# Pooling sums of all four groups on VectorE, issued one by one, and the decay and beta projection in two passes over 32 stationary columns

## The chip, the cores and the metric

The kernel runs on one NeuronCore of a Trainium2 chip. The metric is the device time of one execution in microseconds (us), lower is better. Five engines work in parallel, each through its own instructions in order: PE (TensorE, matrix products), DVE (VectorE), ACT (ScalarE), POOL (GpSimd) and SP (SyncE, which here only issues transfers). An instruction waits where another engine or a transfer has not yet delivered.

## The reference

One transformer-like layer is applied to 128 context tokens and to 1024 latent tokens (a grid of 16 rows by 64 columns). What matters here are two branches of its mixing part, both fed from one normalised and modulated input `h`:

```python
qkv, z, a, b, u, gate_a, gate_b = _split_cols(h @ w_in)
...
g = -jnp.exp(a_log) * jax.nn.softplus(a4 + dt_bias)   # log-decay, 8 columns of the projection
beta = jax.nn.sigmoid(b4)                             # 8 more columns
...
for gi, w in enumerate(POOL_WINDOWS):                 # windows 2, 4, 8, 16
    ug = uf[:, :, gi]                                 # 128 channels each
    if grid_w is None:
        m = _window_mean(ug, w, 1)
    else:
        m = _window_mean(_window_mean(grid, w, 2), w, 1)
    outs.append(m - ug)
y = jnp.einsum('btgc,gcd->btgd', d, w_pool)
```

The pooling branch takes, for each of four groups of 128 channels, the mean over a centred window (along the context sequence, and along both axes of the latent grid), subtracts the value itself, and multiplies by a 128 by 128 matrix per group. The decays and the betas are 16 columns of the same input projection. All tensors are 32-bit floats.

## The kernel before, in words

All 1152 tokens lie along the free axis of tiles of 128 channels, in three chunks of 384 tokens. A product of 32-bit precision is made from three matmuls in a faster format: each operand is split into a rounded part and a rest (`hi`, `lo`), and hi times hi, hi times lo and lo times hi are added in PSUM (`gemm`, lines 499 to 501). A split is an ACT copy (`whi`, L157) and a subtraction on DVE (`wlo`, L158). Three PSUM banks (`psg`, tag "g") take the chunks in turn; a chunk's matmuls wait until the evacuation of the chunk three before it is done.

The order on every engine is the order in which the Python code issues instructions. `gemm_stream` gives the order of the products that the prediction speaks of: the pooling inputs `u` of groups 3, 2, 1, 0 (`u_task`), the decay and beta projection (`ab_task`), q, k and v of head 0 (`conv_task`, each 24 steps of three matmuls, with a five-tap convolution on DVE behind it), the pooling projection (`pool_proj`), and then the product of its result with `w_b_proj` (`yb_task`). After the products for groups 1 and 0, for ab, q, k and v stands a modulation step (`with_mod`: `mod_step`, 16 matmuls of a vector with a part of `w_mod`, L386; DVE copies its result to `part`, L388). Then SP loads the next part of `w_mod` (four transfers of 512 KB, tile `wm`, L264) into the same four tiles. Behind the projection of ab two small matmuls (`modr`, L409) make a row that DVE finishes in four operations (`gra`, L411 and L412) and SP stores (`grow_d`, L413); the next four `wm` loads stand behind that store in SP's queue.

VectorE work that has no fixed place waits in a queue `bg`: every second step of a `gemm` takes one entry from its front and issues it. The pooling sums of groups 2, 1 and 0 (windows 8, 4, 2) are such entries, the convolution taps are appended behind them (L541). A group's sums are doublings: two zeroed pads and a copy, then log2(window) additions, for the context, for two halves of the grid along the columns, and for two halves along the rows; then a product with the reciprocal counts (`rc`, loaded by SP, L602; L630) and the subtraction of the input. Group 3 (window 16) instead is issued at once, all 35 instructions, on GpSimd (`pool_group(g, u, POOL, now)`). `pool_split` makes `dh` and `dl` of a group's result; `pool_proj` drains the queue until three groups are split, splits group 3, and multiplies the groups in the order 2, 1, 0, 3: 12 chunks of three matmuls, evacuated by `scaled` in turn by ACT (L193) and by DVE (L198, tile `sp`).

Of the kernel before, what the change touches and what calls it, by code (L numbers as in the profile page):

```python
# [79 lines left out]
def hybrid_layer(ctx: ExitStack, tc: tile.TileContext, ins, outs, dbg=None):  # L80
# [66 lines left out]
    def w_split():  # L147
        i = wstate["split"]
        if i >= len(wq):
            return  # L150
        while wstate["raw"] <= i:
            w_load()
        wstate["split"] += 1
        t, n = wraw.pop(i)
        hi = wts.tile([P, 1024], F32R, tag="hi", bufs=2, name=f"whi{i}")
        lo = wts.tile([P, 1024], F32R, tag="lo", bufs=2, name=f"wlo{i}")
        ACT.activation(out=hi[:, 0:n], in_=t[:, 0:n], func=AF.Copy)  # L157
        lo_eng[0].tensor_tensor(out=lo[:, 0:n], in0=t[:, 0:n], in1=hi[:, 0:n].bitcast(F32), op=ALU.subtract)  # L158
        wsplit[i] = (hi, lo)
# [79 lines left out]
    with tc.manual_schedule():  # L239
# [276 lines left out]
        def conv_task(dst, m):  # L516

            pb = pad[pad_i[0] % 2]
            pad_i[0] += 1
            taps[m] = 4  # L520

            def evac(c, o):
                if c == 0:
                    while old and taps[old]:
                        bg.popleft()()
                    ACT.copy(out=pb[:, 2:130], in_=o[:, 0:128])
                    ACT.copy(out=pb[:, 132:388], in_=o[:, 128:384])
# [42 lines left out]
        d_act = {}  # L570
        d_raw = {}

        def window_sum(q, x, y, n, w, pos, out):

            p = w // 2
            a, b = x, y
            v = 2
            while v <= w:
                r = w // 2 - v // 2
                s, e = p - r, p + n + r  # L580
                d = v // 4
                lo, hi = (s - 1, s) if v == 2 else (s - d, s + d)
                o = out if v == w else pos(b, s, e)
                q("tensor_tensor", out=o, in0=pos(a, lo, lo + e - s), in1=pos(a, hi, hi + e - s), op=ALU.add)
                a, b = b, a
                v *= 2

        def pool_group(g, u, eng, queue):
            w = WINDOWS[g]
            p = w // 2  # L590

            def q(f, **kw):
                queue.append(lambda: getattr(eng, f)(**kw))

            rcb = []
            s = slot(name="plS")
            t0 = slot(name="plA")
            t1 = slot(name="plB")

            def rc_load():  # L600
                rcb.append(slot(name="rc"))
                SP.dma_start(out=rcb[0][:, 0:T], in_=I["rc"][g:g + 1].to_broadcast([P, T]))  # L602

            def pads(lo, hi, **kw):
                def f():
                    eng.memset(lo, 0.0)
                    eng.memset(hi, 0.0)
                    eng.tensor_copy(**kw)
                queue.append(f)

            pads(t0[:, 0:p], t0[:, p + T_CTX:p + T_CTX + p], out=t0[:, p:p + T_CTX], in_=u[:, 0:T_CTX])
            window_sum(q, t0, t1, T_CTX, w, lambda t, a, b: t[:, a:b], s[:, 0:T_CTX])
            LW = GRID_W + w
            for half in range(2):
                nr = GRID_H // 2
                a0 = T_CTX + half * nr * GRID_W
                va, vb = v3(t0, nr, LW), v3(t1, nr, LW)
                pads(va[:, :, 0:p], va[:, :, p + GRID_W:LW], out=va[:, :, p:p + GRID_W], in_=v3(u, nr, GRID_W, a0))
                window_sum(q, va, vb, GRID_W, w, lambda t, a, b: t[:, :, a:b], v3(s, nr, GRID_W, a0))
            LH = GRID_H + w  # L620
            grid = v3(s, GRID_H, GRID_W, T_CTX)
            for half in range(2):
                ncol = GRID_W // 2
                va, vb = v3(t0, LH, ncol), v3(t1, LH, ncol)
                cs = slice(half * ncol, (half + 1) * ncol)
                if half == 1:
                    queue.append(rc_load)
                pads(va[:, 0:p], va[:, p + GRID_H:LH], out=va[:, p:p + GRID_H, :], in_=grid[:, :, cs])
                window_sum(q, va, vb, GRID_H, w, lambda t, a, b: t[:, a:b, :], grid[:, :, cs])
            queue.append(lambda: eng.tensor_tensor(out=s[:, 0:T], in0=s[:, 0:T], in1=rcb[0][:, 0:T], op=ALU.mult))  # L630
            q("tensor_tensor", out=s[:, 0:T], in0=s[:, 0:T], in1=u[:, 0:T], op=ALU.subtract)
            d_raw[g] = s
            if eng is DVE:

                queue.append(lambda: queue.insert(min(12, len(queue)), lambda: pool_split(g)))

        def pool_split(g):
            s = d_raw.pop(g)
# [4 lines left out]
        def u_task(g, early=None):  # L643
            u = slot(name="u")

            def evac(c, o):
                ACT.copy(out=u[:, c * CH:(c + 1) * CH], in_=o)

            if early is None:
                yield from gemm(8, h_at, evac)  # L650
            else:
                w, acc = early
                for c, o in enumerate(acc):
                    evac(c, o)
# [12 lines left out]

        abt = []

        def ab_task():  # L670
            abt.append(slot(name="ab"))
            abs_ = abt[0][0:16]

            def evac(c, o):
                ACT.copy(out=abs_[:, c * CH:(c + 1) * CH], in_=o)

            yield from gemm(8, h_at, evac, m=16)

        gcol = {}
        gc_d = dram.tile([72, P], F32, name="gc_d")  # L680

        def gate_prep(fill):
            pt = psd("abT")
            abs_ = abt.pop()[0:16]
            for c in range(NT):
                PE.transpose(pt[:, c * 16:(c + 1) * 16], abs_[:, c * P:(c + 1) * P], ident[0:16, 0:16])
# [4 lines left out]
            ab = pt[:, 0:144].rearrange("p (c j) -> p j c", j=16)  # L691

            def col(name):
                t = const.tile([P, 72], F32, name=name)
# [7 lines left out]
            xa, ax, e, s2, q, t1 = (gp[:, 72 * i:72 * i + 72] for i in range(6))  # L702
            sums, gr = gp[:, 432:432 + 3 * P], gp[0:72, 816:816 + P]
            SP.dma_start(out=sums, in_=I["sums"])
            beta = col("beta")
            fill(2500)
            DVE.tensor_tensor(out=w3(xa), in0=ab[:, 0:8, :], in1=bc_last(dtb, NT), op=ALU.add)
# [1587 lines left out]
```

## Time and profile before

| | |
|---|---|
| median of 3 runs | 1802.12 us (1800.2 to 1806.25) |
| profiled execution, its own time | 1805.9 us |
| span of that execution in the trace | 1804.1 us |
| PE busy, share of the span | 93% |
| DVE, ACT, POOL busy | 64%, 40%, 42% |
| mean granted clock of PE | 0.972 of full speed |

All positions in time below are microseconds from the start of the span. The profiled execution took 1.8 us more than its span, and 3.8 us more than the median of the runs. A busy PE means that matmuls overlap without a gap in the trace; whether it advances at full speed is seen from the distance between the starts of two matmuls.

### The profile page before, as it was taken

How to read it: one execution, taken by the hardware profiler on the slowest of the kernel's cores; microseconds unless marked ns; L12 is line 12 of the kernel's file. 1: busy time of each engine (PE TensorE's matmuls, PEld its weight loads, DVE VectorE, ACT ScalarE, POOL GpSimd, SP SyncE). 2: the span in 40 equal slices, each digit the busy share in tenths (PEclk: the TensorE clock that was granted, in tenths of full speed). 3: DMA queues.
4: the chain of work that ended last, by engine and by line, in shares of the span. 5: the costliest groups of instructions: out<-in, count | busy, mean ns of one | idle time of the engine just before them, and what ended most of it. 6: DMA issues, size and time to landing. Idle time of an engine off the chain costs nothing.

```text
span 1804.1 us, 26141 instructions
## 1 busy us (share of the span) xinstructions
PE 1684.0 (93%) x10127; PEld 1534.9 (85%) x10127; DVE 1146.2 (64%) x1963; ACT 729.7 (40%) x1403; POOL 758.3 (42%) x551
## 2 busy tenths in 40 slices
PE   5999999999999899988897899999999999998995
PEld 4877998889999899887676799999999998686774
DVE  4697546568468468458567655555555556457688
ACT  4313652363463363233355433333333333345453
POOL 0350222323333243056101466666666653164875
PEclk9999999999999999999998899999999999999997
DMA  9344442214214213453453022222222234652244
GB/s 321 97 151 170 138 122 81 66 41 123 83 40 126 65 49 118 157 184 108 148 179 117 13 91 91 91 91 91 91 91 91 91 114 164 225 166 94 82 164 169
DMA packets 173309, 211.61 MB, mean 117 GB/s; under 512 B 34877, under 2 KB 118294, under 8 KB 173186
## 3 DMA queue, kind: packets, MB, share of 16 engines
q1 hardware_dynamic: 139676, 180.71, 30.1%
q10 hardware_dynamic: 31205, 19.80, 3.8%
q0 software_dynamic: 2304, 9.44, 1.5%
q8 instruction: 79, 1.29, 0.3%
q14 instruction: 45, 0.36, 0.1%
HBM read 159.99 MB, written 49.93 MB: 116 GB/s over the span
## 4 chain that ended last, share of the span: by engine, by line
PE 46%; DVE 13%; ACT 4%; issue 4%; POOL 2%; DMA 2%; SPq 0%; DVEq 0%; ACTq 0%; POOLq 0%
PE m L1786 5%; PE m L1785 5%; PE m L1784 5%; PE c L1830 3%; PE c L1829 3%; PE c L1831 3%; PE dn L2131 3%; PE dn L2129 3%; PE dn L2130 3%; DVE WD L876 2%; PE g L499 2%; DVE XB L878 1%; PE g L500 1%; PE g L501 1%; PE o L1518 1%
## 5 line engine op out<-in xcount | busy, mean ns | idle before, releaser
L499 PE MATMUL g<-hh,whi 128*128 128x384 f32 (+1 forms) x848 | 309.6, 365 | 1.6 <-ACT sga L1221 1.6
L501 PE MATMUL g<-hh,wlo 128*128 128x384 f32 (+1 forms) x848 | 289.4, 341 | 0.0
L500 PE MATMUL g<-hl,whi 128*128 128x384 f32 (+1 forms) x848 | 287.6, 339 | 0.0
L158 POOL TENSOR_TENSOR wlo<-wraw,whi 128x1024 fp32r<-128x1024 f32 (+2 forms) x42 | 87.4, 2082 | 304.6 <-ACT whi L157 246.7
L499 PEld LDWEIGHTS g<-hh,whi 128*128 128x128 f32 (+1 forms) x848 | 159.9, 189 | 10.6 <-issue 3.4
L180 DVE TENSOR_TENSOR ulo<-wsum,uhi 128x1024 fp32r<-128x1024 f32 (+1 forms) x56 | 100.2, 1790 | 103.0 <-ACT uhi L179 100.5
L500 PEld LDWEIGHTS g<-hl,whi 128*128 128x128 f32 (+1 forms) x848 | 160.5, 189 | 1.8
L501 PEld LDWEIGHTS g<-hh,wlo 128*128 128x128 f32 (+1 forms) x848 | 159.3, 188 | 1.9
L1831 PE MATMUL c<-h3h,ulo 128*128 128x384 f32 x352 | 119.3, 339 | 2.7 <-DVE ulo L180 2.7
L1713 POOL TENSOR_TENSOR wsum<-wr,wr 128x512 f32<-128x512 f32 x63 | 101.9, 1639 | 46.8 <-DMA wr<-in_w_up_dram 46.8
L1829 PE MATMUL c<-h3h,uhi 128*128 128x384 f32 x352 | 119.4, 339 | 0.0
L1830 PE MATMUL c<-h3l,uhi 128*128 128x384 f32 x352 | 119.3, 339 | 0.0
L180 DVE TENSOR_TENSOR ulo<-wr,uhi 128x512 fp32r<-128x512 f32 x92 | 94.2, 1063 | 33.2 <-ACT uhi L179 33.2
L179 ACT ACTIVATE uhi<-wsum 128x1024 fp32r<-128x1024 f32 (+1 forms) x56 | 57.4, 1026 | 132.8 <-PE c L1830 50.3
L2131 PE MATMUL dn<-wdhi,fl 128*128 128x512 f32 x264 | 104.2, 395 | 1.2 <-DVE fl L180 1.2
L2130 PE MATMUL dn<-wdlo,fh 128*128 128x512 f32 x264 | 104.0, 394 | 1.3 <-DVE wdlo L180 1.3
L2129 PE MATMUL dn<-wdhi,fh 128*128 128x512 f32 x264 | 104.6, 396 | 0.0
L1713 POOL TENSOR_TENSOR wsum<-wr 128x512 f32<-128x512 f32 x43 | 57.9, 1356 | 102.5 <-DVE wlo L158 93.5
L1784 PE MATMUL m<-oah,uhi 128*128 128x384 f32 x260 | 88.8, 341 | 5.7 <-ACT sgu L1796 5.7
L1784 PE MATMUL m<-obh,uhi 128*128 128x384 f32 x260 | 88.8, 341 | 1.4 <-ACT uhi L179 1.4
L1922 POOL TENSOR_TENSOR ws<-wd,wd 128x512 f32<-128x512 f32 x33 | 60.2, 1847 | 69.6 <-DVE wdlo L180 51.0
L1786 PE MATMUL m<-obh,ulo 128*128 128x384 f32 x260 | 88.8, 341 | 0.3 <-DVE ulo L180 0.2
(447 smaller groups left out, 4599.9 us busy)
## 6 DMA issues: line engine op xcount, KB each, us to landing
wm<-in_w_mod_dram SPq DMA_DIRECT2D x48, 512.0 KB
wr<-in_w_up_dram SPq DMA_DIRECT2D x44, 512.0 KB
fr<-fo_d SPq DMA_DIRECT2D x35, 512.0 KB
wraw<-in_w_in_dram ACTq DMA_DIRECT2D x26, 512.0 KB
fo_d<-fs SPq DMA_DIRECT2D x22, 512.0 KB
wd<-in_w_down_dram SPq DMA_DIRECT2D x44, 256.0 KB
wraw<-in_w_o_dram SPq DMA_DIRECT2D x20, 512.0 KB
fo_d<-sgu SPq DMA_DIRECT2D x11, 512.0 KB
```

The source lines that it names most:

```text
L180: eng.tensor_tensor(out=lo, in0=src, in1=hi.bitcast(F32), op=ALU.subtract)
L499: PE.matmul(o, wh, a_hi, start=(k == 0), stop=False)
L500: PE.matmul(o, wh, a_lo, start=False, stop=False)
L501: PE.matmul(o, wl, a_hi, start=False, stop=(k == nk - 1))
L1713: eng.tensor_tensor(out=v3(s, 4, P, 512 * i), in0=w_block(u, a), in1=w_block(u, b), op=op)
L1784: PE.matmul(o, wh[:, ks], bh, start=(kp == 0), stop=False)
L1786: PE.matmul(o, wl[:, ks], bh, start=False, stop=(kp == 3))
L1829: PE.matmul(o, wh[:, ks], bh, start=(k == 0), stop=False)
L1830: PE.matmul(o, wh[:, ks], bl, start=False, stop=False)
L1831: PE.matmul(o, wl[:, ks], bh, start=False, stop=(k == 7))
L2129: PE.matmul(o, fh[:, fs], wh[:, w], start=(j == 0), stop=False)
L2131: PE.matmul(o, fl[:, fs], wh[:, w], start=False, stop=(j == NJ - 1))
```

## The change

All four groups go through `bg` on VectorE. A group is one queue entry that holds a generator: each time it is taken it issues the next operation and puts itself back at the front, so one group is finished before the next begins, and its tiles are taken and its `rc` load is issued only when it comes to them. The split of a group is issued at the eighth step of the next group; the last group's is inserted up to eight entries behind its end. `pool_proj` waits for four groups and takes them in the order 3, 2, 1, 0. A test that treated tile number 0 as "no tile" now drains the taps of q before v's first chunk is evacuated. For the decay and beta projection the 16 columns of `hi` and of `lo` are interleaved into one stationary operand of 32 columns, multiplied with both parts of `h`; 16 rows of the result are added to the other 16 after the transposition.

```diff
@@ w_split
+        if n == P:
+            v, t = (x[:, 0:w].rearrange("p (k n) -> p k n", k=8) for x, w in ((hi, 2 * P), (t, P)))
+            ACT.activation(out=v[:, :, 0:16], in_=t, func=AF.Copy)
+            lo_eng[0].tensor_tensor(out=v[:, :, 16:32], in0=t, in1=v[:, :, 0:16].bitcast(F32), op=ALU.subtract)
...
@@ conv_task, evac
-                    while old and taps[old]:
+                    while old is not None and taps[old]:
                         bg.popleft()()
...
@@ pool_group
-            def q(f, **kw):
-                queue.append(lambda: getattr(eng, f)(**kw))
...
-                if half == 1:
-                    queue.append(rc_load)
+                if half == 1:
+                    rc = slot(name="rc")
+                    SP.dma_start(out=rc[:, 0:T], in_=I["rc"][g:g + 1].to_broadcast([P, T]))
...
+        def pool_group(g, u):
+            ops = pool_ops(g, u)
+            n = [0]
+            def step():
+                n[0] += 1
+                if n[0] == 8 and d_raw:
+                    pool_split(min(d_raw))
+                if next(ops, 0) is None:
+                    bg.appendleft(step)
+                elif g == GORD[-1]:
+                    bg.insert(min(8, len(bg)), lambda: pool_split(g))
+            bg.append(step)
...
@@ u_task
-            if g == 3:
-                now = deque()
-                pool_group(g, u, POOL, now)
-                while now:
-                    now.popleft()()
-            else:
-                pool_group(g, u, DVE, bg)
+            pool_group(g, u)
...
@@ ab_task
-            yield from gemm(8, h_at, evac, m=16)
+            hl, _ = w_get()
+            for c in range(NCH):
+                o = psg()[0:32, 0:CH]
+                for k in range(8):
+                    w = hl[:, k * 32:(k + 1) * 32]
+                    for i, a in enumerate(h_at(k, c)):
+                        PE.matmul(o, w, a, start=(k + i == 0), stop=(k + i == 8))
...
@@ gate_prep
+            ACT.copy(out=ab, in_=both[:, 16:32])
+            DVE.tensor_tensor(out=ab, in0=both[:, 0:16], in1=ab, op=ALU.add)
...
@@ pool_proj
-            while len(d_act) < 3:
+            while len(d_act) < 4:
                 bg.popleft()()
...
-            pool_split(3)
-            for g in (2, 1, 0, 3):
+            for g in GORD:
```

Three places show how the instructions move. The first is PE at the start of the decay and beta projection: `hh` and `hl` are the two parts of the input, `whi` and `wlo` the two parts of the weights, `g` the PSUM bank. Before:

```order
L386 MATMUL mod_1015<-wm_697,cT 32x512 x2
L499 MATMUL g_1030<-hh_240,whi_919 16x384
L500 MATMUL g_1030<-hl_241,whi_919 16x384
L501 MATMUL g_1030<-hh_240,wlo_920 16x384
L499 MATMUL g_1030<-hh_245,whi_919 16x384
```

And now:

```order
L393 MATMUL mod_987<-wm_697,cT 32x512 x2
L689 MATMUL g_1002<-hh_240,whi_884 32x384
L689 MATMUL g_1002<-hl_241,whi_884 32x384
L689 MATMUL g_1002<-hh_245,whi_884 32x384
L689 MATMUL g_1002<-hl_246,whi_884 32x384
```

Two matmuls now stand for three, 48 in place of 72 over the projection. The second place is SP's queue from the load of the counts of group 1 to the products' weights behind the modulation step after k (`rc` are the counts, `wraw` raw weights, `wm` the four tiles of `w_mod`). Before:

```order
L144 DMA wraw_1331<-in_w_b_proj_dram 128x4x128
L602 DMA rc_1333<-in_rc_dram 128x1152
L264 DMA wm_694<-in_w_mod_dram 128x2x512
L264 DMA wm_695<-in_w_mod_dram 128x2x512
L264 DMA wm_696<-in_w_mod_dram 128x2x512
L264 DMA wm_697<-in_w_mod_dram 128x2x512
L144 DMA wraw_1461<-in_w_b_proj_dram 128x4x128
```

And now:

```order
L628 DMA rc_1256<-in_rc_dram 128x1152
L144 DMA wraw_1291<-in_w_b_proj_dram 128x4x128
L271 DMA wm_694<-in_w_mod_dram 128x2x512
L271 DMA wm_695<-in_w_mod_dram 128x2x512
L271 DMA wm_696<-in_w_mod_dram 128x2x512
L271 DMA wm_697<-in_w_mod_dram 128x2x512
L628 DMA rc_1402<-in_rc_dram 128x1152
L144 DMA wraw_1441<-in_w_b_proj_dram 128x4x128
```

The counts of the last group (`rc_1333`, now `rc_1402`) stood ahead of the four loads and now stand behind them. The third place is DVE around the same modulation step and up to the splits for the pooling projection (`plS` a group's sums, `qkv` with `pad_151` the taps of q and with `pad_152` those of k, `dl` a group's split, `part` the copy after a modulation step). Before:

```order
L630 TENSOR_TENSOR plS_1012<-plS_1012,rc_1333 128x1152
L180 TENSOR_TENSOR dl_1367<-plS_893,dh_1366 128x1152
L593 TENSOR_TENSOR plS_1012<-plS_1012,u_911 128x1152
L541 SCALAR_TENSOR_TENSOR qkv_1162<-pad_151,ccol,qkv_1162 128x1154
L397 TENSOR_TENSOR A_162<-modc_1392,vcol 128x16
L423 TENSOR_SCALAR A_162<-A_162 128x16
L424 TENSOR_TENSOR A_162<-A_162,vcol 128x16
L388 COPY part_1404<-mod_1405 128x512
L158 TENSOR_TENSOR wlo_1428<-wraw_1211,whi_1427 128x512
L541 SCALAR_TENSOR_TENSOR qkv_1162<-pad_151,ccol,qkv_1162 128x1154 x3
L180 TENSOR_TENSOR dl_1464<-plS_1012,dh_1463 128x1152
L541 SCALAR_TENSOR_TENSOR qkv_1284<-pad_152,ccol,qkv_1284 128x1154 x4
```

And now:

```order
L395 COPY part_1371<-mod_1372 128x512
L165 TENSOR_TENSOR wlo_1395<-wraw_1166,whi_1394 128x512
L187 TENSOR_TENSOR dl_1399<-plS_1140,dh_1398 128x1152
L597 MEMSET plA_1301 128x32
L598 MEMSET plA_1301 128x32
L599 COPY plA_1301<-plS_1300 128x512
L591 TENSOR_TENSOR plS_1300<-plA_1301 128x16x32
L632 TENSOR_TENSOR plS_1300<-plS_1300,rc_1402 128x1152
L634 TENSOR_TENSOR plS_1300<-plS_1300,u_876 128x1152
L548 SCALAR_TENSOR_TENSOR qkv_1114<-pad_151,ccol,qkv_1114 128x1154 x4
L548 SCALAR_TENSOR_TENSOR qkv_1244<-pad_152,ccol,qkv_1244 128x1154 x3
L187 TENSOR_TENSOR dl_1473<-plS_1300,dh_1472 128x1152
```

The last group's product with its counts has moved from ahead of the modulation step's copy to behind it, and all eight taps of q and k now stand behind that product; before, one tap stood ahead of the copy. Behind the rows shown, DVE then issues in both kernels a copy `part`, one more split (before, group 3's) or one more tap (now), and `sp`, its first evacuation of the pooling projection.

## Rows read from the trace of the kernel before

**Rows 1.** The page, its busy line (us, share of the span, instructions).
```profile
PE 1684.0 (93%) x10127; PEld 1534.9 (85%) x10127; DVE 1146.2 (64%) x1963; ACT 729.7 (40%) x1403; POOL 758.3 (42%) x551
```

**Rows 2.** Timeline of PE, the pooling projection (start us, us, engine line op).
```profile
171.39 0.44 PE L1185 MATMUL g<-dh,whi 128*128 128x384 f32 x1
...
177.17 0.69 PE L1185 MATMUL g<-dh,whi 128*128 128x384 f32 x1 [2.87 <-DVE sp L198]
...
177.66 0.52 PE L1186 MATMUL g<-dl,whi 128*128 128x384 f32 x1
...
177.98 0.52 PE L1187 MATMUL g<-dh,wlo 128*128 128x384 f32 x1
```

**Rows 3.** Window of that stage: PE, PEld, DVE, ACT, POOL busy, PEclk, DMA, GB/s.
```profile
175.00:180.00 5.00, 2.83 (x9) 2.63 (x10) 3.82 (x6) 2.66 (x6) 1.38 (x2) 0.58 0.12 29
```

**Rows 4.** Timeline of DVE: beside GpSimd, then the chain before the pooling projection.
```profile
74.95 1.39 DVE L158 TENSOR_TENSOR wlo<-wraw,whi 128x1024 fp32r<-128x1024 f32 x1 [2.60 <-ACT whi L157]
...
104.45 2.41 DVE L593 TENSOR_TENSOR plB<-plA 128x704 f32<-128x704 f32 x1
...
142.12 1.36 DVE L630 TENSOR_TENSOR plS<-plS,rc 128x1152 f32<-128x1152 f32 x1 [6.30 <-DMA rc<-in_rc_dram]
...
153.56 1.36 DVE L630 TENSOR_TENSOR plS<-plS,rc 128x1152 f32<-128x1152 f32 x1 [1.70 <-DMA rc<-in_rc_dram]
...
160.41 4.33 DVE L541 SCALAR_TENSOR_TENSOR qkv<-pad,ccol,qkv 128x1154 f32<-128x1154 f32 x3
...
176.51 0.60 DVE L198 TENSOR_SCALAR sp<-g,vcol 128x384 f32<-128x384 f32 x1
```

**Rows 5.** Timeline of PE, the modulation steps before k and before v.
```profile
136.01 1.60 PE L386 MATMUL mod<-wm,cT 128*32 128x512 f32 x8
...
139.51 1.05 PE L386 MATMUL mod<-wm,cT 128*32 128x512 f32 x4 [0.45 <-DMA wm<-in_w_mod_dram]
...
140.50 0.44 PE L499 MATMUL g<-hh,whi 128*128 128x384 f32 x1
...
154.93 1.92 PE L386 MATMUL mod<-wm,cT 128*32 128x512 f32 x16
...
156.78 0.44 PE L499 MATMUL g<-hh,whi 128*128 128x384 f32 x1
```

**Rows 6.** Timeline of SP (SPq: the DMA queue's issues), the loads behind them.
```profile
130.90 0.23 SPq L413 DMA_DIRECT2D grow_d<-gra  x1
...
131.23 1.92 SPq L264 DMA_DIRECT2D wm<-in_w_mod_dram  x4
...
133.65 0.35 SPq L602 DMA_DIRECT2D rc<-in_rc_dram  x1
...
148.75 0.50 SPq L602 DMA_DIRECT2D rc<-in_rc_dram  x1
...
156.02 2.27 SPq L264 DMA_DIRECT2D wm<-in_w_mod_dram  x4
```

**Rows 7.** Timeline of PE, the decay and beta projection, up to q.
```profile
106.62 0.34 PE L499 MATMUL g<-hh,whi 128*16 128x384 f32 x1
...
118.95 0.34 PE L501 MATMUL g<-hh,wlo 128*16 128x384 f32 x1
...
120.58 0.59 PE L409 MATMUL modr<-part,cst 128*2 128x512 f32 x1 [0.34 <-DVE part L388]
...
123.25 0.45 PE L499 MATMUL g<-hh,whi 128*128 128x384 f32 x1
```

**Rows 8.** DVE groups by shape, 114 to 157 us (us, mean ns | idle before).
```profile
L630 DVE TENSOR_TENSOR plS<-plS,rc 128x1152 f32<-128x1152 f32 x3 | 4.1, 1359 | 8.0 <-DMA rc<-in_rc_dram 8.0
...
L593 DVE TENSOR_TENSOR plB<-plA 128x704 f32<-128x704 f32 x1 | 0.9, 891 | 0.0
```

**Rows 9.** Window of POOL's pooling, first to last instruction: busy, PEclk, DMA.
```profile
72.10:114.40 42.30, 40.42 (x35) 1.00 0.47 154
```

**Rows 10.** Window of DVE, group 2 beside GpSimd: busy us, PEclk, DMA.
```profile
81.00:119.92 38.92, 38.10 (x36) 1.00 0.45 151
```

More of the change, by code (lines that the diff above doesn't have):

```diff
@@ L156, in w_split @@
         lo = wts.tile([P, 1024], F32R, tag="lo", bufs=2, name=f"wlo{i}")
+        if n == P:
+            v, t = (x[:, 0:w].rearrange("p (k n) -> p k n", k=8) for x, w in ((hi, 2 * P), (t, P)))
+            ACT.activation(out=v[:, :, 0:16], in_=t, func=AF.Copy)
+            lo_eng[0].tensor_tensor(out=v[:, :, 16:32], in0=t, in1=v[:, :, 0:16].bitcast(F32), op=ALU.subtract)
+            wsplit[i] = (hi, lo)
+            return
         ACT.activation(out=hi[:, 0:n], in_=t[:, 0:n], func=AF.Copy)
@@ L571, in hybrid_layer, with window_sum @@
         d_raw = {}
-        def window_sum(q, x, y, n, w, pos, out):
+        def window_sum(x, y, n, w, pos, out):
             p = w // 2
@@ L583, in window_sum, with pads, pool_ops @@
                 o = out if v == w else pos(b, s, e)
-                q("tensor_tensor", out=o, in0=pos(a, lo, lo + e - s), in1=pos(a, hi, hi + e - s), op=ALU.add)
+                DVE.tensor_tensor(out=o, in0=pos(a, lo, lo + e - s), in1=pos(a, hi, hi + e - s), op=ALU.add)
+                yield
                 a, b = b, a
                 v *= 2
-        def pool_group(g, u, eng, queue):
+        def pads(lo, hi, **kw):
+            DVE.memset(lo, 0.0)
+            DVE.memset(hi, 0.0)
+            DVE.tensor_copy(**kw)
+        def pool_ops(g, u):
             w = WINDOWS[g]
             p = w // 2
-            def q(f, **kw):
-                queue.append(lambda: getattr(eng, f)(**kw))
-            rcb = []
             s = slot(name="plS")
@@ L598, in pool_group @@
             t1 = slot(name="plB")
[L600 to L609, printed above, removed]
             pads(t0[:, 0:p], t0[:, p + T_CTX:p + T_CTX + p], out=t0[:, p:p + T_CTX], in_=u[:, 0:T_CTX])
-            window_sum(q, t0, t1, T_CTX, w, lambda t, a, b: t[:, a:b], s[:, 0:T_CTX])
+            for _ in window_sum(t0, t1, T_CTX, w, lambda t, a, b: t[:, a:b], s[:, 0:T_CTX]):
+                pass
+            yield
             LW = GRID_W + w
@@ L618, in pool_group @@
                 pads(va[:, :, 0:p], va[:, :, p + GRID_W:LW], out=va[:, :, p:p + GRID_W], in_=v3(u, nr, GRID_W, a0))
-                window_sum(q, va, vb, GRID_W, w, lambda t, a, b: t[:, :, a:b], v3(s, nr, GRID_W, a0))
+                yield
+                yield from window_sum(va, vb, GRID_W, w, lambda t, a, b: t[:, :, a:b], v3(s, nr, GRID_W, a0))
             LH = GRID_H + w
@@ L626, in pool_group @@
                 if half == 1:
-                    queue.append(rc_load)
+                    rc = slot(name="rc")
+                    SP.dma_start(out=rc[:, 0:T], in_=I["rc"][g:g + 1].to_broadcast([P, T]))
                 pads(va[:, 0:p], va[:, p + GRID_H:LH], out=va[:, p:p + GRID_H, :], in_=grid[:, :, cs])
-                window_sum(q, va, vb, GRID_H, w, lambda t, a, b: t[:, a:b, :], grid[:, :, cs])
-            queue.append(lambda: eng.tensor_tensor(out=s[:, 0:T], in0=s[:, 0:T], in1=rcb[0][:, 0:T], op=ALU.mult))
-            q("tensor_tensor", out=s[:, 0:T], in0=s[:, 0:T], in1=u[:, 0:T], op=ALU.subtract)
-            d_raw[g] = s
-            if eng is DVE:
-                queue.append(lambda: queue.insert(min(12, len(queue)), lambda: pool_split(g)))
+                yield
+                yield from window_sum(va, vb, GRID_H, w, lambda t, a, b: t[:, a:b, :], grid[:, :, cs])
+            DVE.tensor_tensor(out=s[:, 0:T], in0=s[:, 0:T], in1=rc[:, 0:T], op=ALU.mult)
+            yield
+            DVE.tensor_tensor(out=s[:, 0:T], in0=s[:, 0:T], in1=u[:, 0:T], op=ALU.subtract)
+            d_raw[g] = s
+        def pool_group(g, u):
[10 more added lines that the diff above has]
+            bg.append(step)
         def pool_split(g):
@@ L671, in ab_task @@
             abt.append(slot(name="ab"))
-            abs_ = abt[0][0:16]
-            def evac(c, o):
-                ACT.copy(out=abs_[:, c * CH:(c + 1) * CH], in_=o)
-            yield from gemm(8, h_at, evac, m=16)
+            hl, _ = w_get()
[5 more added lines that the diff above has]
+                        PE.matmul(o, w, a, start=(k + i == 0), stop=(k + i == 8))
+                    if k == 1:
+                        if c == 0:
+                            w_ahead()
+                        elif c == 1:
+                            w_more()
+                    bg_n[0] += 1
+                    if bg and bg_n[1] and bg_n[0] % bg_n[1] == 0:
+                        bg.popleft()()
+                    yield 350
+                ACT.copy(out=abt[0][0:32, c * CH:(c + 1) * CH], in_=o)
         gcol = {}
@@ L683, in gate_prep @@
             pt = psd("abT")
-            abs_ = abt.pop()[0:16]
+            abs_ = abt.pop()[0:32]
             for c in range(NT):
-                PE.transpose(pt[:, c * 16:(c + 1) * 16], abs_[:, c * P:(c + 1) * P], ident[0:16, 0:16])
+                PE.transpose(pt[:, c * 32:(c + 1) * 32], abs_[:, c * P:(c + 1) * P], ident[0:32, 0:32])
             dtb = const.tile([P, 8], F32, name="dtb")
@@ L690, in gate_prep @@
             SP.dma_start(out=alg, in_=I["a_log"].rearrange("o d h -> o (d h)").to_broadcast([P, 8]))
-            ab = pt[:, 0:144].rearrange("p (c j) -> p j c", j=16)
             def col(name):
@@ L704, in gate_prep @@
             SP.dma_start(out=sums, in_=I["sums"])
+            ab = gp[:, 944:944 + 16 * NT].rearrange("p (j c) -> p j c", c=NT)
+            both = pt[:, 0:32 * NT].rearrange("p (c j) -> p j c", j=32)
+            ACT.copy(out=ab, in_=both[:, 16:32])
+            DVE.tensor_tensor(out=ab, in0=both[:, 0:16], in1=ab, op=ALU.add)
             beta = col("beta")
```

## The prediction, made before the change was run

> **What bounds the kernel now.** I read the page first: PE is busy 93% of the span, DVE 64% [rows 1]. So the end moves where PE is delivered earlier or has less to do, and DVE's added work counts only where PE waits for it. The change touches nothing before the sums begin at about 76 us and nothing behind the pooling projection's evacuations, except that everything later may shift as a whole. I therefore went through PE's timeline from 100 to 190 us and asked at each gap what ended it.
>
> The largest gap is in the pooling projection. It starts at 171.39, and at its fifth chunk PE has waited 2.87 us for DVE's tile `sp`, until 177.17; behind that the starts of two matmuls lie 0.32 us apart (177.66, 177.98) [rows 2], and the granted clock of that stretch is 0.58 [rows 3], partly the lower level of 1.2 GHz; elsewhere here it is 2.4 GHz. DVE reaches that `sp` only at 176.51: before it, in its order, stand the product with the counts of group 0 (153.56, after a wait for `rc`), taps, splits and a copy [rows 4]. Reckoned from the start of v on PE, 156.78 [rows 5], `sp` comes 19.7 us later.
>
> The second gap is the modulation step ahead of k. An undisturbed step takes 1.85 us (154.93 to 156.78); this one takes 4.49 (136.01 to 140.50), with waits for the loads `wm`: 2.64 us lost [rows 5]. Those loads were issued from 131.23 only, right behind the store `grow_d` at 130.90, which waits for DVE's row operations [rows 6]. So here too the cause is DVE, through SP's queue. A third gap, 0.34 us, is again a wait for DVE's `part` [rows 7].
>
> **The projection of ab.** Its 72 matmuls take from 106.62 to 118.95 between the first and the last start: 12.33 / 71 = 0.174 us each, with 16 columns [rows 7]. I take the same for 32 columns, since the 128-column product behind it has the same spacing in the timeline. 24 fewer give 24 x 0.174 = 4.2 us. One ACT copy and one DVE addition of 144 columns come in, into the evacuations of the pooling projection: about 0.3 us each, and DVE's is on the path there: +0.3 us.
>
> **Group 3 on DVE.** From 114 to 157 us DVE works without GpSimd: a sum over 704 columns takes 0.89 us, one over 1152 takes 1.36 [rows 8], so 1.05 ns for each further column. Beside GpSimd the same 704 columns took 2.41 us [rows 4]. Group 3 has per half 624, 608, 576, 512 columns and 960, 896, 768, 512, by that slope 0.81, 0.79, 0.76, 0.69 and 1.16, 1.09, 0.96, 0.69; both halves 13.9 us; four context sums 1.2, copies and pads 3.2, the two operations over all tokens 2.7: 21 us. The lower bound is this, the upper one the 42.3 us from GpSimd's first to its last pooling instruction [rows 9]. I take 21, because GpSimd now does nothing there. For the same reason group 2, which took 38.9 us beside GpSimd (81.0 to 119.9, two other short operations in it) [rows 10], shrinks to 15.4 by the same reckoning. What is added is nearly what is saved: 21 + 15 against 37.
>
> **When DVE reaches the row operations.** DVE starts the sums at 76.3, when the split of 74.95 is done [rows 4]. Up to the row operations stand group 3 (21), group 2 without its last two operations (12.7), splits and copies (about 5.2), waits for PE's modulation step and for the counts of group 3 behind its `wm` loads (taken as 3.5), the four row operations (2.6): 121.3. In the trace it was 130.9 [rows 6]. PE finishes ab 4.2 us earlier, loses the 0.34 no more, and starts q at 123.25 - 4.5 = 118.75; q ends 12.76 later, at 131.5. The loads then go out from about 121.7 and need some 8.3 us (131.23 to the last wait's end at 139.51) [rows 5, 6]: 130.0, before they are wanted. So the 2.64 us go too, with about 2 us to spare. v starts 4.2 + 0.3 + 2.6 = 7.1 us earlier, at 149.7.
>
> **Where it is given back.** The counts of group 0 are now issued behind the four `wm` loads of the step ahead of v. Those loads begin 0.76 us before v starts (156.02 against 156.78) and take 2.27 us to issue [rows 5, 6], so `rc` goes out at v + 1.5. How long it then takes is bounded by two rows: with nothing ahead of it, 4.8 us (148.75 to 153.56); behind four `wm` loads, 8.5 us (133.65 to 142.12) [rows 4, 6]. The second is the same situation, and I take it: `rc` lands at v + 10.0. DVE is there before: copy, split of weights, split of group 1 and one more half are 3.7 us after the copy, and the copy is at most 2 us late.
>
> The Trainium skill (DMA: Bandwidth & Descriptors, Queues, rings and completion order) says that the transfers of one issuing queue are started in ring order on each DMA engine, while their completions are not promised in order. By that rule a load that stands behind 2 MB has to let them start first, which speaks against this change and agrees with the 8.5 us row; without it the 4.8 us would stand and the sum would be 3.7 us lower.
>
> From v + 10.0 DVE has the product and the subtraction (2.7 us), seven taps at 4.33 / 3 = 1.44 us (10.1), group 0's split (1.3, as an operation of 1152 columns), the eighth tap (1.45) and a copy of 512 columns (0.6) [rows 4, 8]: `sp` at v + 26.1. It was v + 19.7. The evacuations, two chunks in some 1.7 to 1.9 us, then go on as before. So 26.1 - 19.7 = 6.4 us of the 7.1 are lost, and 0.3 for the addition.
>
> **The sum.** -7.1 + 6.4 + 0.3 = -0.4 us; 1805.9 becomes 1805.5, and as the profiled execution lay 3.8 us above the median of the runs, the median becomes 1801.7. Behind the projection the order of all engines is the old one, so I take the shift to last to the end. Bounds: `rc` in 4.8 us gives -4.1, thus 1798.0; if the loads ahead of k are late after all, v gains only 4.5 and the sum is +2.2, thus 1804.3; taps slowed by GpSimd's splits, as the neighbouring rows of DVE bear out, another 1 us, 1805.3.
>
> **Rivals.**
> (a) The counts are not held up: 1798.0. For it: one `rc` landed in 4.8 us. Against: that one had no load ahead of it.
> (b) The gain ahead of v is kept: the taps or other parts of the chain shrink so that `sp` stays at v + 19.7. Then 1802.1 - 7.1 + 0.3 = 1795.3. For it: DVE as a whole has no more work than before. Against: the chain from the last counts on is 16 us by rows in which GpSimd hardly disturbs.
> (c) Slower, by TensorE's clock. PE is idle for longer ahead of `sp` (v's first bank is not evacuated before q's taps are done, at v + 18.5, when PE has finished v and its step at v + 14.6). In the trace the clock is low behind the wait [rows 2, 3], while the projection is paced by DVE anyway. If it stays low into the next product, each matmul costs 0.32 - 0.174 = 0.146 us more; 37 of them reach the 0.3% bound, 72 (two output tiles of that product) give +10.5: 1812. Against: over the whole span the mean granted clock is 0.972, so low stretches are short.
> The Trainium skill (TensorE: Matmul & The Clock Gate, HAM oscillation) describes matmul bursts with waits between them that start at the halved clock each time; the trace agrees so far, with its clock of 0.58 behind a 2.87 us wait.
> (d) The sums stay as slow on DVE as they were beside GpSimd, so that nothing is relieved. 2.41 / 0.89 = 2.7 times 36 us would bring DVE to the row operations some 60 us late, and PE would wait for `wm` about 50 us: 1850. Against: the same sums are fast as soon as GpSimd stops.
>
> **Numbers.** My forecast, gained and given back, 0.63; (a) 0.12; (b) 0.13; (c) 0.10; (d) 0.02. Two executions of one kernel differ by up to 6 us here, and 0.3% is 5.4 us: about what a measurement can tell from no change. (b) is faster by over 0.3%, (c) and (d) slower; the forecast and (a) lie mostly within, with 0.03 beyond on either side. So faster 0.16, within 0.3% 0.69, slower 0.15. The range for 8 in 10 takes in (a), the bounds and the scatter, down to about half of the way to (b), and leaves out (c) and (d): 1796.5 to 1807.
>
> **What would show it.** In the changed kernel: ab in 48 matmuls at 0.174 us; no pooling on POOL; 704-column sums at 0.9 us throughout; the step ahead of k without a wait for `wm`; v on PE at about 150; the last product with the counts idle for `rc` some 4 to 5 us; and a longer idle time of PE ahead of and in the pooling projection, whose `sp` comes at about 176. If that product does not wait, the forecast is wrong towards (a) or (b); if PE's starts behind the projection lie 0.32 us apart, towards (c); if the step ahead of k still waits, DVE is slower than reckoned.

## The result, and the profile after

The change makes the kernel slower: 1811.13 us median of six runs (1808.88 to 1821.53) against 1801.85 us (1800.08 to 1806.25) for the kernel before on the same chip, ratio 1.0057 with a 95% interval of 1.0041 to 1.0072. The profiled execution took 1810.42 us, its span is 1808.6 us. The forecast was 1801.7 us, with a range up to 1807.

Start-up differs by some 3 us between profiled executions, before anything that was changed. So positions are compared from the split `wlo` that stands ahead of the sums on DVE: at 74.95 in the kernel before [rows 4], at 72.97 in the changed one.

Most of what was predicted up to v is there. The page's busy line of the changed kernel, to be held against [rows 1]:

```profile
PE 1672.9 (92%) x10103; PEld 1527.6 (84%) x10103; DVE 1143.6 (63%) x2001; ACT 729.5 (40%) x1404; POOL 718.3 (40%) x514
```

POOL lost 37 instructions, DVE has 38 more and is busy for no longer. The reason is in DVE's groups by shape between 70 and 150 us (busy us, mean ns | idle before): the same 704 columns that took 2.41 us beside GpSimd [rows 4] now take 0.89.

```profile
L591 DVE TENSOR_TENSOR plB<-plA 128x960 f32<-128x960 f32 x2 | 2.3, 1158 | 0.1
L591 DVE TENSOR_TENSOR plA<-plB 128x896 f32<-128x896 f32 x2 | 2.2, 1092 | 0.1
...
L591 DVE TENSOR_TENSOR plB<-plA 128x704 f32<-128x704 f32 x2 | 1.8, 892 | 0.1
```

PE's timeline of the changed kernel (start us, us): the projection of ab with its first and last matmul, the modulation step ahead of k with the first matmul behind it, the first matmul of v, v's modulation step, and the pooling projection.

```profile
104.64 0.37 PE L689 MATMUL g<-hh,whi 128*32 128x384 f32 x1
...
112.85 0.34 PE L689 MATMUL g<-hl,whi 128*32 128x384 f32 x1
...
129.40 1.92 PE L393 MATMUL mod<-wm,cT 128*32 128x512 f32 x16
131.26 0.44 PE L506 MATMUL g<-hh,whi 128*128 128x384 f32 x1
...
147.56 0.44 PE L506 MATMUL g<-hh,whi 128*128 128x384 f32 x1
...
160.31 1.92 PE L393 MATMUL mod<-wm,cT 128*32 128x512 f32 x16
175.11 0.69 PE L1209 MATMUL g<-dh,whi 128*128 128x384 f32 x1 [12.87 <-ACT pad L534]
...
176.24 0.52 PE L1209 MATMUL g<-dh,whi 128*128 128x384 f32 x1
176.56 0.52 PE L1210 MATMUL g<-dl,whi 128*128 128x384 f32 x1
...
183.54 0.69 PE L1209 MATMUL g<-dh,whi 128*128 128x384 f32 x1 [3.01 <-DVE sp L205]
```

The 48 matmuls of ab start 8.21 / 47 = 0.175 us apart. From the start of the step ahead of k to the next product pass 1.86 us, without a wait, where it was 4.49 [rows 5]. v starts 74.6 us behind `wlo`; it was 81.8 [rows 4, 5], so 7.2 us are gained (7.1 predicted). Then PE, which waited 2.87 us in and none ahead of the pooling projection [rows 2], waits 12.87 us ahead of it and 3.01 us in it. The first of these waits is for ACT's copy of v's first bank, and ACT's timeline shows that this copy waits for taps on DVE:

```profile
174.52 0.27 ACT L533 COPY pad<-g 128x128 f32<-128x128 f32 x1 [27.00 <-DVE qkv L548]
```

DVE's timeline shows what holds up the taps (168.58) and `sp`:

```profile
72.97 1.23 DVE L165 TENSOR_TENSOR wlo<-wraw,whi 128x1024 fp32r<-128x1024 f32 x1 [2.60 <-ACT whi L164]
...
142.19 1.36 DVE L632 TENSOR_TENSOR plS<-plS,rc 128x1152 f32<-128x1152 f32 x1 [6.22 <-DMA rc<-in_rc_dram]
...
150.09 0.68 DVE L165 TENSOR_TENSOR wlo<-wraw,whi 128x512 fp32r<-128x512 f32 x1
161.47 1.36 DVE L187 TENSOR_TENSOR dl<-plS,dh 128x1152 fp32r<-128x1152 f32 x1 [10.70 <-PE mod L393]
...
165.91 1.36 DVE L632 TENSOR_TENSOR plS<-plS,rc 128x1152 f32<-128x1152 f32 x1 [1.96 <-DMA rc<-in_rc_dram]
...
168.58 10.17 DVE L548 SCALAR_TENSOR_TENSOR qkv<-pad,ccol,qkv 128x1154 f32<-128x1154 f32 x7
178.66 1.35 DVE L187 TENSOR_TENSOR dl<-plS,dh 128x1152 fp32r<-128x1152 f32 x1
179.93 2.43 DVE L548 SCALAR_TENSOR_TENSOR qkv<-pad,ccol,qkv 128x1154 f32<-128x1154 f32 x1
182.28 0.68 DVE L395 COPY part<-mod 128x512 f32<-128x512 f32 x1
182.88 0.60 DVE L205 TENSOR_SCALAR sp<-g,vcol 128x384 f32<-128x384 f32 x1
```

The split `dl` of group 1 is the new thing. It reads `plS` and `dh`, both ready by 147.5 (ACT's `dh` starts at 146.38 and takes 1.15), and yet DVE stands idle for 10.70 us until a matmul of the modulation step behind v, "v's modulation step", on PE. SP shows the same moment. In its queue the counts of group 0 stand right behind the four `wm` loads, and go out 12.77 us after the last of these was issued, at 161.47, as the split starts:

```profile
120.21 0.23 SPq L420 DMA_DIRECT2D grow_d<-gra  x1
120.54 1.93 SPq L271 DMA_DIRECT2D wm<-in_w_mod_dram  x4
...
132.98 0.51 SPq L628 DMA_DIRECT2D rc<-in_rc_dram  x1
...
146.80 1.90 SPq L271 DMA_DIRECT2D wm<-in_w_mod_dram  x4
...
161.47 0.35 SPq L628 DMA_DIRECT2D rc<-in_rc_dram  x1
```

Neither reads anything of that step. What ties them to it is where their tiles lie. All such tiles come from one pool of 35 buffers (`slots`), and the program puts the new ones into the buffers of the four `wm` tiles. The assignment, read from the built program (new tile, whose buffer it takes, the last reader that it must wait for):

```
dl_1399 (group 1)    wm_694    PE, v's modulation step
rc_1402 (group 0)    wm_695    PE, v's modulation step
dh_1472 (group 0)    wm_696    PE, v's modulation step
dl_1473 (group 0)    wm_697    PE, v's modulation step
before: dh_1463      plS_893   DVE, the split of group 1
before: dl_1464      part_1147 PE, products ahead of v
```

At that point every other buffer is in use: 16 of `h`, 2 pads, 4 `wm`, 4 with the splits of groups 3 and 2, 3 with sums of groups 1 and 0, the `dh` of group 1, the outputs of q and k, ab, `part` and the input of group 0, 35 together. In the kernel before, 32 were in use when the last split (group 0's) took its two buffers, so three were free. One of the three is group 3, which lay there as one raw sum instead of two split halves until the projection; the other two are the input and one of the sums of group 0, which was done with its sums by then and now is not.

### The profile page after: what moved, and what is told of

It reads as the page before. It is cut to its first block, busy times and chain, and to the rows that moved or that the text cites. A ratio compares the mean times of both kernels' runs of the same rounds, so it can differ in the third digit from the quotient of the medians.

```text
span 1808.6 us, 26098 instructions
## 1 busy us (share of the span) xinstructions
PE 1672.9 (92%) x10103; PEld 1527.6 (84%) x10103; DVE 1143.6 (63%) x2001; ACT 729.5 (40%) x1404; POOL 718.3 (40%) x514
## 4 chain that ended last, share of the span: by engine, by line
PE 45%; DVE 12%; ACT 4%; issue 4%; POOL 3%; DMA 2%; SPq 0%; DVEq 0%; ACTq 0%; POOLq 0%
PE m L1810 5%; PE m L1808 5%; PE m L1809 5%; PE c L1855 3%; PE c L1854 3%; PE c L1853 3%; PE dn L2155 3%; PE dn L2153 3%; PE dn L2154 3%; PE g L506 2%; DVE WD L901 2%; DVE XB L903 2%; PE g L508 2%; PE g L507 2%; DVE fl L187 1%
## 5 line engine op out<-in xcount | busy, mean ns | idle before, releaser
L506 PE MATMUL g<-hh,whi 128*128 128x384 f32 x824 | 302.4, 367 | 1.6 <-ACT sga L1245 1.6
L508 PE MATMUL g<-hh,wlo 128*128 128x384 f32 x824 | 281.8, 342 | 0.0
L507 PE MATMUL g<-hl,whi 128*128 128x384 f32 x824 | 280.1, 340 | 0.0
L506 PEld LDWEIGHTS g<-hh,whi 128*128 128x128 f32 x824 | 158.2, 192 | 7.9 <-issue 2.5
L507 PEld LDWEIGHTS g<-hl,whi 128*128 128x128 f32 x824 | 158.9, 193 | 0.0
L508 PEld LDWEIGHTS g<-hh,wlo 128*128 128x128 f32 x824 | 157.5, 191 | 0.0
L1810 PE MATMUL m<-oah,ulo 128*128 128x384 f32 x260 | 88.7, 341 | 0.0
```

The lines of the kernel that those rows point to most:

```text
L506: PE.matmul(o, wh, a_hi, start=(k == 0), stop=False)
L507: PE.matmul(o, wh, a_lo, start=False, stop=False)
L508: PE.matmul(o, wl, a_hi, start=False, stop=(k == nk - 1))
L1810: PE.matmul(o, wl[:, ks], bh, start=False, stop=(kp == 3))
```

## The experiments

Theory 1: the pool of 35 is full, so the split and the counts wait for v's modulation step, and with them everything behind them on DVE. Theory 2: as predicted, the counts are late because they stand behind four weight loads in SP's queue. Theory 3: the amount of work on DVE. Theory 4: the low clock of the pooling projection. Theory 5: the new rule that forces q's taps ahead of v's first evacuation. e1 to e4, e5 to e8 and e9 to e11 each share a chip with runs of the kernel before (medians 1804.48, 1802.83 and 1803.01 us). A ratio is estimated from all runs of its chip and need not be the quotient of two medians: those of e4 give 1.0050, its ratio is 1.0055.

| run | median us | ratio to before (95%) | v from `wlo` | `sp` from v | `sp` from `wlo` | end of span from `wlo` |
|---|---|---|---|---|---|---|
| before | 1801.85 | 1 | 81.8 | 19.7 | 101.6 | 1729.1 |
| after | 1811.13 | 1.0057 (1.0041 to 1.0072) | 74.6 | 35.3 | 109.9 | 1735.6 |
| e1 two extra buffers | 1804.16 | 1.0003 (0.9994 to 1.0012) | 74.6 | 26.8 | 101.4 | 1729.1 |
| e2 and counts early | 1800.71 | 0.9978 (0.9969 to 0.9988) | 74.6 | 20.8 | 95.4 | 1725.9 |
| e3 before, ab in two passes | 1804.26 | 0.9999 (0.9990 to 1.0008) | 81.6 | 17.7 | 99.3 | 1729.1 |
| e4 after, ab in three | 1813.53 | 1.0055 (1.0040 to 1.0070) | 78.7 | 35.2 | 113.9 | 1735.7 |
| e5 one extra buffer | 1813.03 | 1.0056 (1.0041 to 1.0070) | 74.6 | 33.4 | 108.0 | 1735.6 |
| e6 before, three tiles held | 1810.14 | 1.0040 (1.0024 to 1.0055) | 81.8 | 25.5 | 107.3 | 1735.1 |
| e7 no forced taps | 1812.28 | 1.0054 (1.0039 to 1.0069) | 74.6 | 33.1 | 107.7 | 1733.0 |
| e8 before, counts early | 1802.10 | 0.9994 (0.9983 to 1.0005) | 80.7 | 17.7 | 98.4 | 1722.4 |
| e9 e2, ab in three | 1803.53 | 1.0002 (0.9990 to 1.0014) | 78.7 | 20.8 | 99.5 | 1730.6 |
| e10 e8, ab in two | 1803.84 | 1.0009 (0.9997 to 1.0020) | 80.7 | 17.7 | 98.4 | 1730.0 |
| e11 e2, ACT evacuates | 1798.51 | 0.9973 (0.9961 to 0.9985) | 74.6 | 21.2 | 95.8 | 1728.6 |

The last four columns are differences of two times in one profiled execution. What is faster or slower is read from the ratios, since the end of one execution scatters (e8's span is 6.7 us shorter, its ratio 0.9994). `sp` is DVE's first evacuation of the projection; in e11 it belongs to a later chunk than in the other rows.

**e1, two extra buffers.** A small pool lies in the space that the delta rule's tiles take over later.

```diff
-    dn = dn_pool.enter_context(tc.tile_pool(name="dn", bufs=1))
+    dn = [dn_pool.enter_context(tc.tile_pool(name="early", bufs=1))]   # closed, and "dn" opened, after yb
...
-            abt.append(slot(name="ab"))
+            abt.append(spare("ab"))
...
-                    rc = slot(name="rc")
+                    rc = spare("rc")
```

> The changed kernel, with the ab tile and the counts held in two extra buffers laid where the delta rule's small tiles lie later, so that the pool of 35 tiles has room. Theory 1 (the pool of 35 is full; the split of group 1 and the counts of group 0 wait until v's modulation step gives its four weight tiles back, 10.7 us of idle DVE): that split follows its group's subtraction at about v + 3, the counts are asked for at v + 1.5 and sp comes at v + 22 to v + 26 instead of v + 35.3, so 9 to 13 us less than the changed kernel: 1798 to 1802. Theory 2 (as predicted, the counts stand behind four weight loads in SP's queue and that alone costs): also at v + 26 and 1802, but the wait for the counts is the 6 us one and DVE's idle time goes to it. Theory 3 (the sums' amount of work on DVE) and theory 4 (the low clock of the pooling projection): no change, 1809 to 1812.

The loss is gone: 1.0003. The time itself, 1804.16 us, lies above the 1798 to 1802 expected, on a chip where the kernel before takes 1804.48. DVE's and SP's timelines, v starting at 149.85:

```profile
152.05 1.35 DVE L191 TENSOR_TENSOR dl<-plS,dh 128x1152 fp32r<-128x1152 f32 x1
...
159.66 1.36 DVE L636 TENSOR_TENSOR plS<-plS,rc 128x1152 f32<-128x1152 f32 x1 [5.14 <-DMA rc<-in_rc_dram]
...
176.63 0.60 DVE L209 TENSOR_SCALAR sp<-g,vcol 128x384 f32<-128x384 f32 x1
```

```profile
149.09 1.90 SPq L275 DMA_DIRECT2D wm<-in_w_mod_dram  x4
151.08 0.61 SPq L632 DMA_DIRECT2D rc<-in_rc_dram  x1
```

The split no longer waits, the counts go out at v + 1.2, DVE has them at v + 9.8, and `sp` comes at v + 26.8. Theories 3 and 5 fall: the work and the forced taps are those of the changed kernel. Theory 4 falls too: in e1 the pooling projection still runs at the lower clock, and more of it than in the changed kernel. 21 of its 36 matmuls have the next start 0.32 us behind their own, 15 in the changed kernel, 14 in the kernel before. PE's timeline of e1, behind the wait ahead of the projection:

```profile
168.86 0.62 PE L1213 MATMUL g<-dh,whi 128*128 128x384 f32 x1 [4.33 <-ACT pad L538]
169.28 0.52 PE L1214 MATMUL g<-dl,whi 128*128 128x384 f32 x1
169.60 0.52 PE L1215 MATMUL g<-dh,wlo 128*128 128x384 f32 x1
```

What is left is the wait of theory 2, 5.14 us.

**e2, the counts early too** (the edit against e1).

```diff
             t1 = slot(name="plB")
+            rc = spare("rc")
+            SP.dma_start(out=rc[:, 0:T], in_=I["rc"][g:g + 1].to_broadcast([P, T]))
...
-                if half == 1:
-                    rc = spare("rc")
-                    SP.dma_start(out=rc[:, 0:T], in_=I["rc"][g:g + 1].to_broadcast([P, T]))
```

> The kernel of the run before this one, with the counts of each group asked for when the group's first sum is issued, so ahead of the four weight loads. Theory 1 alone: the counts were not what DVE waited for once the tiles are there: the same within 1 us. Theory 2 on top of it: the product with the counts of group 0 stops waiting and sp comes 3 to 6 us earlier: 3 to 6 us below the run before, 1793 to 1799.

Theory 2 holds on top of theory 1. DVE's and SP's timelines, v starting at 148.40:

```profile
152.27 1.36 DVE L635 TENSOR_TENSOR plS<-plS,rc 128x1152 f32<-128x1152 f32 x1
...
169.23 0.60 DVE L209 TENSOR_SCALAR sp<-g,vcol 128x384 f32<-128x384 f32 x1
```

```profile
137.74 0.35 SPq L613 DMA_DIRECT2D rc<-in_rc_dram  x1
147.63 1.90 SPq L275 DMA_DIRECT2D wm<-in_w_mod_dram  x4
```

The product does not wait, `sp` comes 6.0 us earlier than in e1, and the medians differ by 3.45 us. This kernel is faster than the one before, 0.9978.

**e3 and e4, the two parts alone.** In e3 only the projection of ab is changed, in e4 only the pooling (the other part is the text of the kernel before).

```diff
-            yield from gemm(8, h_at, evac, m=16)
+            hl, _ = w_get()     # e3: two passes in the kernel before; e4: the reverse in the changed one
```

> The kernel before, with the ab projection in two passes and nothing else changed: group 3 stays on GpSimd. If DVE sets the pace up to the row operations there, the 4.2 us saved on PE come back as a longer wait for the weight tiles ahead of k: within 1 us of the kernel before, 1801 to 1803. If PE's own work sets the pace: 4 us less, 1797.5.

> The changed kernel with the ab projection in three passes as before, so the change of the pooling alone. Theory 1 (DVE is held until v's modulation step on PE): v and all behind it start 4.2 us later, 1815. Theory 3 (DVE's amount of work sets the time): the wait in the pooling projection shrinks by as much, 1811.

e3 is the first case: 0.9999. PE's timeline shows what was saved again at the row behind ab, as a wait of 4.43 us for DVE's copy, where [rows 7] has 0.34 us:

```profile
117.75 0.76 PE L416 MATMUL modr<-part,cst 128*2 128x512 f32 x1 [4.43 <-DVE part L395]
```

e4 missed what theory 1 expected of the time. v and `sp` are 4.1 and 4.0 us later than in the changed kernel, as expected, but the end of the span is not. By the trace those 4 us are given back in the delta rule: its transpositions start at 244.1 (after) and 249.5 (e4), and its last ones at 672.6 and 671.5. In the first head's stage e4 had the full granted clock and the changed kernel had not. Windows of the changed kernel (us, PE busy, PEclk, DMA, GB/s; the first is in the pooling projection), then of e4:

```profile
175.00:180.00 5.00, 4.05 (x11) 0.50 0.00 0
...
300.00:350.00 50.00, 43.46 (x448) 0.86 0.29 76
```

```profile
300.00:350.00 50.00, 44.05 (x482) 1.00 0.32 87
```

This is one execution of each. Whether the medians agree for the same reason stays open.

**e5, one extra buffer.** As e1, but ab stays in the pool of 35.

```diff
-                    rc = slot(name="rc")
+                    rc = spare("rc")
```

> The changed kernel with one extra buffer instead of two: the counts alone are held outside the pool of 35, ab stays in it. Theory 1: the pool is still full when group 1 is split, so DVE still waits for v's modulation step (to about v + 14) before that split; only the counts are there by then, and the 2.0 us wait of the product behind it goes: sp at v + 33, 2 us below the changed kernel. If it was the counts' own late issue that cost (a variant of theory 2): sp at v + 26 and the time of the kernel before, 1.000.

As theory 1 said: the counts go out early, at v + 1.2, the split still waits (DVE's timeline), `sp` is at v + 33.4, and of its 1.9 us the ratio shows nothing (1.0056). So the wait of the split costs the time even where the counts have room, and the variant with the counts falls. The reverse, room for the split alone, was not run. By the changed kernel's rows it need not help: the counts go out at 161.47, the product with them starts 4.4 us later, and no split would have brought it forward.

```profile
163.69 1.36 DVE L191 TENSOR_TENSOR dl<-plS,dh 128x1152 fp32r<-128x1152 f32 x1 [11.19 <-PE mod L397]
```

**e6, the kernel before with a full pool.** The reverse of e1.

```diff
+            if m == 8:                                   # at the start of v
+                for _ in range(3):
+                    held.append(slot(name="held"))
+                    DVE.memset(held[-1][:, 0:1], 0.0)
...
+            while held:                                  # ahead of the pooling projection
+                DVE.memset(held.pop()[:, 0:1], 1.0)
```

> The kernel before, with three tiles of the pool of 35 taken when v's projection begins and given back ahead of the pooling projection (two tiny writes each on DVE): nothing else is changed. Theory 1: group 0's split then finds no free tile until v's modulation step is done, some 6.5 us later than in the kernel before; sp and the time follow by 5 to 6.5 us: 1.0028 to 1.0036. Theories 2, 3 and 4 (queue order, amount of work, clock): no change, 1.000.

1.0040 (1.0028 to 1.0036 expected, within the interval), `sp` 5.7 us later. The timelines of ACT and DVE show the split of group 0 waiting for the modulation step; the third row is the same split in the kernel before:

```profile
167.96 1.16 ACT L179 ACTIVATE dh<-plS 128x1152 fp32r<-128x1152 f32 x1 [5.65 <-PE mod L386]
```

```profile
169.15 1.36 DVE L180 TENSOR_TENSOR dl<-plS,dh 128x1152 fp32r<-128x1152 f32 x1 [7.47 <-ACT dh L179]
```

```profile
166.46 1.36 DVE L180 TENSOR_TENSOR dl<-plS,dh 128x1152 fp32r<-128x1152 f32 x1 [1.72 <-ACT dh L179]
```

No pooling was moved and no queue reordered here; three idle tiles are enough, as many as were free there.

**e7, no forced taps.**

```diff
-                    while old is not None and taps[old]:
+                    while old and taps[old]:
```

> The changed kernel without the rule that q's remaining taps are issued ahead of the evacuation of v's first bank (its condition written as in the kernel before, where it doesn't hold for that tile). What it leaves out: those taps of head 0 then read v's values instead of q's, so one head's result is another. Theory 5 (it is this forced order that makes PE wait 12.9 us for v's evacuation): the time falls back to that of the kernel before, 1.000. Theory 1: the split and the counts wait as long as in the changed kernel, sp stays at about v + 35, and the time within 2 us of the changed kernel: 1.0045 to 1.0057.

1.0054: theory 5 falls. The split waits 11.09 us, as with the rule.

**e8 to e10, which parts the faster kernel needs.** e8 takes the early counts alone, e10 adds ab in two passes, both with group 3 on GpSimd; e9 is e2 with ab in three passes.

```diff
@@ e8, e10, in the kernel before
-                if half == 1:
-                    queue.append(rc_load)
...
+            queue.append(rc_load)
             pads(t0[:, 0:p], t0[:, p + T_CTX:p + T_CTX + p], out=t0[:, p:p + T_CTX], in_=u[:, 0:T_CTX])
```

> The kernel before, with the counts of each group asked for when its first sum is issued; the pooling of group 3 stays on GpSimd, ab in three passes. Theory 2 for the kernel before: the waits of 6.3 and 1.7 us for the counts go, DVE reaches sp 2 to 8 us earlier, and the wait of 2.9 us and the slow stretch behind it shrink: 2 to 4 us below the kernel before, 0.998 to 0.999. If the waits for the counts were hidden there: 1.000.

> The second run's kernel (two extra buffers, counts asked for early, measured at 0.998), with ab in three passes again. If what PE saves in ab reaches the end once DVE no longer waits for tiles or counts: 4 us slower, 1.000. If it is lost to PE's waits for DVE there too: 0.998.

> The kernel before with the counts asked for early and ab in two passes; the pooling of group 3 stays on GpSimd. If moving group 3 is worth nothing in itself, the same as the second run, 0.998. If DVE's early row operations, which only the move gives, are what lets v start 7 us earlier: about 0.9994 to 1.000, as with the early counts alone.

With early counts DVE's waits of 6.30 and 1.70 us [rows 4] are gone in e8 and `sp` comes 3.2 us earlier, but no time is shown to be gained (0.9994, the interval holds 1). e10 gains nothing more, since v starts as late as in e8. e9 loses e2's gain (1.0002): its v is 4.1 us later, and here that shows, because neither tiles nor counts hold DVE. So e2's 0.22% needs the pooling on VectorE (e10), early counts (e1) and the shorter ab (e9); that early counts without the two extra buffers would not do was not run.

**e11, a step further.**

```diff
+                    if g == GORD[0] or (g == GORD[1] and c == 0):
+                        turn[0] = 0
                     scaled([(0, CH, vc("pool_scale", g), None)], pt[:, 0:CH], yh[:, cs], yl[:, cs])()
```

> The second run's kernel, with the first four evacuations of the pooling projection scaled on ScalarE instead of every second one on VectorE. There PE waits 3.5 us for VectorE's sp, which stands behind taps and the split of group 0 in VectorE's order. If that wait still sets the end: 2 to 4 us less, 0.996. If what is gained there is absorbed behind the projection, as parts of earlier shifts were: 0.998.

PE's longest wait for DVE's `sp` falls from 3.53 to 0.87 us, and the median is the lowest, 1798.51 us. But 0.9973 and e2's 0.9978 have overlapping intervals, so that this last step gains anything is not shown. Either is faster than the kernel before.

## Why the prediction was wrong, step by step

**What bounds the kernel.** Right. DVE's chain sets the pace twice, at the row operations and at `sp`; e3 shows it from the other side.

**ab: -4.2 us.** Right in size: 0.175 us a matmul, 4.1 us at v (after against e4).

**Group 3 and the row operations.** Right. SP stores the row 47.2 us after `wlo`; predicted were 121.3 - 74.95 = 46.4. The wait ahead of k is gone and v starts 7.2 us earlier. So rival (d), sums that stay slow, falls.

**Where it is given back: the step that failed.** Two sentences were wrong: "so `rc` goes out at v + 1.5" and "DVE is there before". `rc` went out at v + 13.9 and DVE came to its product later still, at v + 16.4, where it waited 1.96 us more for them. The working followed queues and data, and never asked into which buffers the lazily taken tiles would go. Taking them lazily puts the split of group 1 and the counts of group 0 at a time when the weights of v's modulation step hold the last four buffers. `sp` came at v + 35.3 instead of v + 26.1, 9.2 us too late: the sum's +6.4 us was +15.6 (35.3 - 19.7). The forecast missed the median by 9.4 us; that the two agree so closely is in part chance, since e5 and e7 are as slow with `sp` 2 us earlier. e1 gives the two tiles room, leaves the work as it is, and gives the forecast's own numbers: `rc` at v + 9.8 (10.0 predicted), `sp` at v + 26.8 (26.1), no change of the time (-0.4 us predicted, ratio 1.0003 measured). e5, e6 and e7 point the same way.

**The price of standing behind the loads.** Right, and now measured both ways on the same transfer: with nothing ahead of it (after), the product starts 165.91 - 161.47 = 4.4 us after the issue; behind four loads (e1), 159.66 - 151.08 = 8.6 us. The Trainium skill (DMA: Bandwidth & Descriptors, Queues, rings and completion order) says that descriptors are taken in ring order on each DMA engine; the 8.6 us behind four loads against 4.4 agree with that.

**The rivals.** (a), counts not held up, and (b), gain kept, did not happen; e2 comes nearest to (b), with `sp` at v + 20.8, and is worth 0.22%, where (b) had 1795.3 us. (c) named the size, 1812, but not the cause. PE is idle for longer ahead of the projection, and the granted clock behind the wait is 0.50, the lower level (the window of 175 to 180 us, shown with e4); the matmuls start 0.32 us apart as in [rows 2]. But in the next product they are 0.17 us apart (192.68, 192.85, 193.03), and from 200 to 300 us the granted clock is 1.00: the low clock does not persist into that product, which is what (c) needed. And e1, with more matmuls at 0.32 us in the projection, loses nothing.

**What would show it.** The prediction's sign "the last product with the counts idle for `rc` some 4 to 5 us" is 1.96 us in the trace, which it would have read as towards (a) or (b). The idle time had moved to the split ahead of it.

## What to carry to other kernels

An instruction that waits for an engine whose results it does not read may be waiting for a buffer; look up whose buffer its output takes, even where the gap comes once. The Trainium skill (Perfetto Trace Analysis, Optimization Strategy) says that a gap that repeats can mean that there is no room for the next tile; here a single one of 10.7 us meant that. When tiles are taken later or live longer, count what is live at each new moment against the pool, as one counts transfers and instructions: here three more were live than in the kernel before, one through group 3 as two split halves, two through group 0's sums that were still running. And what is saved on an engine that waits may be worth nothing until the wait is moved: the two passes of ab alone gave a ratio of 0.9999, and without them e2's 0.9978 became 1.0002.

## What the runs showed of the hardware

The same sums on DVE took 2.41 us for 704 columns beside GpSimd and 0.89 without it, so 38 more instructions on DVE cost it no busy time over the span (1146.2 us before [rows 1], 1143.6 after).

How much of a shift at `sp` reaches the end was not settled. By the medians, +8.4 us at `sp` in the changed kernel came with +9.3, -6.1 in e2 with -3.8, -2.3 in e3 with none, and the four kernels in which the split of group 1 waits (after, e4, e5, e7) lie within 1.0054 to 1.0057 while their `sp` comes 107.7 to 113.9 us behind `wlo`. In the one trace of e2 a place can be named: the 72 matmuls of `yah` with `whi`, behind the delta rule, take 63.8 us from the first start to the last (759.8 to 823.6), 60.6 in the kernel before (767.8 to 828.4), at a granted clock of 0.89 against 0.97. e2 is 6.9 us ahead of the kernel before, reckoned from `wlo`, where they begin and 3.6 us where they end.
